# An encoder block on one core: a new order of the vector work beside the attention heads, a maximum that begins with the sink, and feed-forward values without the token's scale

## The chip, the core and the metric

The kernel runs on one core of a Trainium2 chip. A core has five engines that run their own instruction streams and wait for each other through semaphores: TensorE (PE in the profile; its weight loads are listed apart as PEld), VectorE (DVE), ScalarE (ACT), GpSimd (POOL) and SyncE (SP), which here only issues DMA transfers. The metric is the device time of one execution in microseconds (us); lower is better. Before the change it is 941.33 us, the median of three runs (941.06 to 941.93).

## The reference

One layer of a bidirectional encoder in float32: 256 tokens of width 2048, 12 query heads and 4 key/value heads of width 128, four Fourier groups, a feed-forward width of 5504. Cut to what matters:

```python
h = rmsnorm(x, norm1_g)
q, k, v, u = split(h @ w_in)
s = q @ k.T * HEAD_DIM**-0.5 - slope[head] * abs(t - s_pos)   # |t - s_pos| <= 128, else -1e30
m = maximum(max(s), sink[head])
p = exp(s - m);  p = p / (sum(p) + exp(sink[head] - m))
a = rmsnorm(p @ v, attn_out_g)
f = rmsnorm(per group: real(fft2(u)) @ w_fourier[g], fourier_out_g)
x = x + concatenate([a, f]) @ w_out

h = rmsnorm(x, norm2_g)
gate, val = split(h @ w_up)
gate = conv3(gate, dw_w) + dw_b           # over three neighbouring tokens, per channel
x = x + (gelu(gate) * val) @ w_down
y = rmsnorm(x, normf_g)
```

An rmsnorm divides each token by the root of its mean square, with 1e-6 added under the root, so a factor of a token's own that reaches the last rmsnorm drops out again, if the 1e-6 is multiplied by the square of that factor.

## The kernel before

**Precision.** Every large product is made of three: each float32 operand is cut into a high and a low part in the type fp32r, and high by high, low by high and high by low are added in PSUM. For the weights this is done while they stream in. `split` (lines 174 to 184) takes one unit of weights, 128 x 2048 numbers: ScalarE writes the high part (L181), VectorE subtracts it from the raw weights for the low part (L182), and the next unit's DMA is issued (L165, L183). There are three buffers each for raw, high and low parts.

**Order of the work.** The order is written out by hand: each engine runs its instructions in the order of the program. `unit` (line 382) is the beat: it runs what was put down as "before" unit i, then the unit's matmuls, then the "beside" list, then the split of unit i+2, then the "behind" list. "Before" holds matmuls only, so on TensorE it comes ahead of the unit's 32 large matmuls. The "beside" list holds VectorE, ScalarE and GpSimd work which in time runs next to the unit's matmuls. On these engines the split of unit i+2 stands behind the whole "beside" list of unit i.

**The stages.** First u and x are loaded and the u projection is made (to about 38 us). Then come the units for v and, from about 53 us, 16 units for keys and queries in the order k, q, q, q for each of the four key heads. In each of these, weights are held still and the tokens' parts move: 16 matmuls of 512 columns and 16 of 256 (L350). Then 16 units of the output projection (to about 251 us), then the feed-forward part.

**A head's way through the units.** If a query head is projected in unit s, then in s+1 its two halves of the PSUM bank are summed (`qk_out`, lines 629 to 636: a ScalarE copy L631 and a VectorE sum L633; for a key head also a product with the token's scale, L635) and cut into parts (`qk_parts`, L642 to 646, through `split_scaled`, L269 on ScalarE and L270 on VectorE). In s+2 TensorE makes the scores (`scores`, L654, ahead of the unit's matmuls), and `scores_out` adds the distances, takes the maximum (L670, VectorE) and makes the exponent's bias `neg` with two GpSimd instructions (L674 product with the token's scale, L675 minimum with the negated sink); `exps` (L684 to 689) follows on ScalarE in the "behind" list, with one small GpSimd sum (L689). In s+3 `weigh` divides (L694, L697), and for the first ten heads `flip_out` transposes blocks of 32 on VectorE (L314) and writes them to HBM in four DMAs (L317). In s+4 `flip_in` reads them back turned (L325). In s+6 `flip_parts` cuts them into parts (L739 ScalarE, L740 VectorE). In s+7 TensorE multiplies with v (`values`, L749), and `values_out` squares the result (L486 ScalarE), cuts it into parts (L269, L270) and adds the squares on GpSimd (L490). The last two heads are turned by TensorE instead (`turn`, `turn_out`).

**The loop that orders it** is in lines 762 to 792. In the "beside" list of one unit it puts, before the change: `flip_parts`, `weigh`, `flip_out`, `flip_in`, `qk_out`, `values_out`, `turn_out`, `scores_out`, `qk_parts`.

**Feed-forward.** Each of the 43 channel tiles has a gate and a value unit. `scaled_sum` (L922 to 926) sums the two halves of the bank and multiplies by `r2b`, the token's scale spread over a row. `gate_conv`, `gate_gelu` and `val_mult` follow. The down-projection's first 36 tiles run as five groups of seven products per column block (a Strassen-like scheme, `PRODUCTS`), whose results are added to x in `xs` by `product_out` (L1118, L1122) and `shared_out` (L1129 to 1141). The last rmsnorm's sums of squares start in `last_post` (L1159 to 1178).

Of the kernel before, what the change touches and what calls it, by code (L numbers as in the profile page):

```python
# [8 lines left out]
F32 = mybir.dt.float32  # L9
F32R = mybir.dt.float32r  # L10
AF = mybir.ActivationFunctionType
ALU = mybir.AluOpType

P = 128
D = 2048
# [3 lines left out]
NH = 12  # L19
# [7 lines left out]
EPS = 1e-6  # L27
# [11 lines left out]
V_G2, V_GA, V_GF, V_DW, V_DB, V_SINK = 0, 16, 28, 32, 161, 204  # L39
V_N = 216  # L40
# [15 lines left out]
FLIPS = range(NH - 2)  # L56
# [48 lines left out]
def block_kernel(  # L105
# [19 lines left out]
    nc = tc.nc  # L125
    SL = slopes()
# [73 lines left out]
    rel = cat_pool.tile([P, 512], F32, tag="cat", name="rel")  # L200
# [59 lines left out]
    ps = bank(dn, "ps_warm")  # L260
# [3 lines left out]
    def vcol(o, n=1):  # L264
        return vec[:, o : o + n]
# [8 lines left out]
    def rstd_of(ssq, width, name, n=2, r=None):  # L274

        var = base.tile([P, n], F32, tag="var" + name, name="var" + name)
        nc.vector.tensor_scalar(var, ssq, 1.0 / width, EPS, ALU.mult, ALU.add)
        if r is None:
            r = base.tile([P, n], F32, tag="rstd" + name, name="rstd" + name)
        nc.gpsimd.tensor_tensor(r, var, half_pow[:, 0:n], ALU.pow)  # L280
        return r
# [7 lines left out]
    def spread(r, dst, name):  # L289

        t = wp.tile([P, 512], F32, tag="junk", name=f"diag{name}")
        dgs = [t[:, b * P : (b + 1) * P] for b in range(2)]
        for b, dg in enumerate(dgs):
            nc.vector.tensor_scalar(dg, ident, r[:, b : b + 1], None, ALU.mult)
        ps = bank(dn, "ps_spread" + name)
        for b in range(2):
            nc.tensor.matmul(
                ps[:, b * P : (b + 1) * P], ones, dgs[b], start=True, stop=True
            )
        nc.vector.tensor_copy(dst, ps[:, :S])  # L300
# [72 lines left out]
    before, beside, behind = {}, {}, {}  # L373

    def at(when, i, f, *a):
        when.setdefault(i, []).append((f, a))
# [13 lines left out]
    for c in range(4):  # L390
        t = base.tile([P, 4, 512], F32R, tag=f"hT{c}", name=f"hT{c}")
        hT.append(t)
    ps_u = [bank(mm, f"ps_u{b}") for b in range(2)]
    for k in range(NK):
# [3 lines left out]
        n = 1 if c < 2 else 2  # L398
# [3 lines left out]
        if q % n == 0:  # L402
            w, h = u_part(k, 0, FW, n), hi[:, q : q + n, :]
# [20 lines left out]
    ph = pa.enter_context(tc.tile_pool(name="pa", bufs=1))  # L424
# [5 lines left out]
    rq_neg = ph.tile([P, 2], F32, tag="rq_neg", name="rq_neg")  # L430
    rq_pos = ph.tile([P, 2], F32, tag="rq_pos", name="rq_pos")
    rq_inv = ph.tile([P, 2], F32, tag="rq_inv", name="rq_inv")
    sink_neg = ph.tile([P, NH], F32, tag="sink_neg", name="sink_neg")

    def token_sums(c):
        for b in range(2):
# [150 lines left out]
    def distances():  # L587

        for b in range(2):
            s = slice(b * S, (b + 1) * S)  # L590
            nc.vector.tensor_scalar(rel[:, s], rel[:, s], rq_inv[:, b : b + 1], None, ALU.mult)
        nc.vector.tensor_scalar(sink_neg, vcol(V_SINK, NH), -1.0, None, ALU.mult)

    at(beside, 5, fourier_positions)
    at(before, 6, fourier_weights)
# [30 lines left out]
    qk_sb, st = {}, {}  # L626
    sq_a = ph.tile([P, S], F32, tag="sq", name="sq_a")

    def qk_out(kind, h, ps):
        tmp = ph.tile([P, S], F32, tag="tmp", name=f"tmp_{kind}{h}", bufs=2)  # L630
        nc.scalar.activation(tmp, ps[:, S : 2 * S], AF.Copy)  # L631
        add = ph.tile([P, S], F32, tag="add", name=f"add_{kind}{h}", bufs=2)
        nc.vector.tensor_tensor(add, ps[:, 0:S], tmp, ALU.add)  # L633
        if kind == "k":
            nc.vector.tensor_tensor(add, add, r1b, ALU.mult)  # L635
        st["add", kind, h] = add
# [25 lines left out]
    def scores_out(h):  # L662

        ps = st.pop(("s", h))
        sc = ph.tile([P, 512], F32, tag="sc", name=f"sc{h}", bufs=4)
        mx = ph.tile([P, 2], F32, tag="mx", name=f"mx{h}", bufs=2)
        neg = ph.tile([P, 2], F32, tag="neg", name=f"neg{h}", bufs=2)
        for b in range(2):
            s = slice(b * S, (b + 1) * S)
            nc.vector.tensor_tensor_reduce(  # L670
                sc[:, s], ps[:, s], rel[:, s], -float(SL[h]), -3e38, ALU.add,
                ALU.max, mx[:, b : b + 1],
            )
        nc.gpsimd.tensor_tensor(neg, mx, rq_neg, ALU.mult)  # L674
        nc.gpsimd.tensor_scalar(neg, neg, sink_neg[:, h : h + 1], None, ALU.min)  # L675
        st["sc", h] = sc, neg

    def exps(h):
# [83 lines left out]
    for i in range(N_QK, N_OUT + 8):  # L762
        heads = {i - s: h for (kind, h), s in slot_of.items() if kind == "q"}
        new = [kh for kh, s in slot_of.items() if i - s == 1]
        for n, h in sorted(heads.items()):
            if n == 5 + 2 * (h in FLIPS):
                at(before, i, values, h)
        if 4 in heads and heads[4] not in FLIPS:
            at(before, i, turn, heads[4])
        if 2 in heads:  # L770
            at(before, i, scores, heads[2])
        if 6 in heads and heads[6] in FLIPS:
            at(beside, i, flip_parts, heads[6])
        if 3 in heads:
            at(beside, i, weigh, heads[3])
            if heads[3] in FLIPS:
                at(beside, i, flip_out, heads[3])
        if 4 in heads and heads[4] in FLIPS:
            at(beside, i, flip_in, heads[4])
        for kind, h in new:  # L780
            at(beside, i, lambda k=kind, h=h: qk_out(k, h, st.pop(("ps", k, h))))
        for n, h in sorted(heads.items()):
            if n == 5 + 2 * (h in FLIPS):
                at(beside, i, values_out, h)
        if 4 in heads and heads[4] not in FLIPS:
            at(beside, i, turn_out, heads[4])
        if 2 in heads:
            at(beside, i, scores_out, heads[2])
        for kind, h in new:
            at(beside, i, qk_parts, kind, h)  # L790
        if 2 in heads:
            at(behind, i, exps, heads[2])

# [85 lines left out]
    for n, (c, kq) in enumerate(OUT_ORDER):  # L879
        i = N_OUT + n  # L880
# [39 lines left out]
    def scaled_sum(ps, name):  # L920
        tmp = fp.tile([P, S], F32, tag="ftmp", name=f"ft_{name}")
        nc.scalar.activation(tmp, ps[:, S : 2 * S], AF.Copy)  # L922
        add = fp.tile([P, S], F32, tag="fadd", name=f"fa_{name}", bufs=3)
        nc.vector.tensor_tensor(add, ps[:, 0:S], tmp, ALU.add)
        nc.vector.tensor_tensor(add, add, r2b, ALU.mult)
        sums_of[name] = add

    def gate_conv(j):
# [182 lines left out]
    def product_out(g, c, p, ps):  # L1111
        tt = nc.vector.tensor_tensor
        if p in ("P6", "P7"):
            z = Z[c, p]
            if g == 0:
                nc.scalar.activation(z, ps, AF.Copy)
            else:
                tt(z, ps, z, ALU.add)  # L1118
        else:
            n, t = {"P2": (0, 0), "N3": (1, 0), "N4": (0, 1)}[p]  # L1120
            xb = xs[2 * n + c][:, t, :]
            tt(xb, ps, xb, ALU.add)  # L1122

    def shared_out(c, step):

        p1, n5, u, p7 = held[c, "P1"], held[c, "N5"], Z[c, "P6"], Z[c, "P7"]
        x00, x10, x01, x11 = (xs[2 * n + c][:, t, :] for n in range(2) for t in range(2))
        tt = nc.vector.tensor_tensor
        if step == 0:  # L1129
            tt(u, p1, u, ALU.add)  # L1130
            tt(x00, p1, x00, ALU.add)
            w = st["w", c] = wp.tile([P, 512], F32, tag="junk", name=f"sum01_{c}")
            tt(w, n5, u, ALU.subtract)
        elif step == 1:
            tt(u, u, p7, ALU.add)
            tt(x01, x01, st["w", c], ALU.add)
            tt(x10, x10, u, ALU.add)
        else:
            w = st.pop(("w", c))
            tt(w, w, p7, ALU.subtract)  # L1140
            tt(x11, x11, w, ALU.add)

    def by_parts(ps, o, hi, lo, n, first, last):

# [14 lines left out]
    def last_post(c, b, ps, o=0, n=512):  # L1159

        xb = xs[c][:, b, o : o + n]
        nc.vector.tensor_tensor(xb, ps, xb, ALU.add)
        if c == 3:
            return
        junk = wp.tile([P, 512], F32, tag="junk", name=f"junkc{c}{b}")
        nc.scalar.activation(
            junk, xb, AF.Square, scale=D**-0.5, accum_out=ssq3[:, b, c : c + 1]
        )
        if c == 0:
            nc.vector.tensor_scalar(  # L1170
                ssq3[:, b, 3:4], ssq3[:, b, 0:1], EPS, None, ALU.add
            )
        if (c, b) == (1, 1):
            nc.gpsimd.tensor_tensor(
                ssq3[:, b, 3:4], ssq3[:, b, 3:4], ssq3[:, b, 1:2], ALU.add
            )
        if (c, b) not in ((1, 1), (2, 1)):
            nc.gpsimd.tensor_tensor(xb, xb, gfb[:, c * 512 : (c + 1) * 512], ALU.mult)
# [34 lines left out]
    for q in range(2):  # L1213
        kind, j = items[q]
# [8 lines left out]
        still_weights(hi, lo, ps, range(12, NK))  # L1223
    tot2 = base.tile([P, 2], F32, tag="tot2", name="tot2")
    nc.vector.tensor_reduce(tot2, ssq2, mybir.AxisListType.X, ALU.add)
    spread(rstd_of(tot2, D, "2"), r2b, "2")
    ff_step(1)
    up_posts(1, *items[0], pair[0][0])
    up_posts(2, *items[1], pair[1][0])
# [208 lines left out]
```

## Time and profile before

| what | value |
|---|---|
| median of three runs | 941.33 us |
| the profiled execution | 941.03 us |
| its span, first to last instruction | 938.9 us |
| busy: TensorE, VectorE, ScalarE, GpSimd | 928.0, 765.5, 539.6, 72.9 us |
| granted TensorE clock, mean over the span | 0.997 of full speed |
| memory | 223.25 MB moved, mean 238 GB/s |

The profiled execution's own time is 2.13 us more than its span; that is what lies around the instructions. In the rows of a timeline the columns are: start in us from the span's beginning, duration in us, engine, line of the kernel, operation, result and operands by the program's names, shape, how many instructions the row merges, and, in brackets, how long the engine sat idle ahead of it and for whom it waited. In a row of a group the numbers after the bar are busy time in us, the mean of one in ns, and idle time ahead of them. A row of busy time by stage gives for PE, PEld, DVE, ACT and POOL the busy us and the number of instructions, then the granted clock, the share of busy DMA engines and GB/s. Matmuls are pipelined and their ends are modelled: their starts are what was recorded, and one's end lies behind the next one's start.

### The profile page before, as it was taken

How to read it: one execution, taken by the hardware profiler on the slowest of the kernel's cores; microseconds unless marked ns; L12 is line 12 of the kernel's file. 1: busy time of each engine (PE TensorE's matmuls, PEld its weight loads, DVE VectorE, ACT ScalarE, POOL GpSimd, SP SyncE). 2: the span in 40 equal slices, each digit the busy share in tenths (PEclk: the TensorE clock that was granted, in tenths of full speed). 3: DMA queues.
4: the chain of work that ended last, by engine and by line, in shares of the span. 5: the costliest groups of instructions: out<-in, count | busy, mean ns of one | idle time of the engine just before them, and what ended most of it. 6: DMA issues, size and time to landing. Idle time of an engine off the chain costs nothing.

```text
span 938.9 us, 12849 instructions
## 1 busy us (share of the span) xinstructions
PE 928.0 (99%) x5005; PEld 803.5 (86%) x5005; DVE 765.5 (82%) x945; ACT 539.6 (57%) x672; POOL 72.9 (8%) x104
## 2 busy tenths in 40 slices
PE   9999999999999999999999999999999999999996
PEld 7888888888888888888888888888888888888885
DVE  7657888778677777798888997878979789989986
ACT  7755666645554555566555665556655556655553
POOL 0102222300000000000000000000000000000002
PEclk9999999999999999999999999999999999999998
DMA  9965767557757668887797778777787978779652
GB/s 367 309 224 169 231 196 236 193 174 281 243 221 232 177 227 238 278 269 239 220 296 252 246 216 286 237 262 232 260 248 240 309 224 269 241 233 273 194 179 90
DMA packets 55148, 223.25 MB, mean 238 GB/s; under 512 B 21136, under 2 KB 25744, under 8 KB 31536
## 3 DMA queue, kind: packets, MB, share of 16 engines
q1 hardware_dynamic: 50544, 192.94, 56.8%
q0 software_dynamic: 4544, 29.49, 16.9%
q8 instruction: 39, 0.64, 0.3%
q14 instruction: 21, 0.17, 0.1%
HBM read 216.13 MB, written 6.29 MB: 237 GB/s over the span
## 4 chain that ended last, share of the span: by engine, by line
PE 95%; DVE 2%; ACT 1%; issue 1%; DMA 0%; POOL 0%; DVEq 0%; POOLq 0%; ACTq 0%
PE ps_val L350 25%; PE ps_gate L350 25%; PE ps_q L350 5%; PE ps_P L1148 3%; PE ps_P L1149 3%; PE ps_P L1147 3%; PE ps_N L1148 3%; PE ps_N L1149 3%; PE ps_N L1147 3%; PE ps_k L350 2%; PE ps_a L333 2%; PE ps_a L335 2%; PE ps_a L334 2%; PE ps_s L654 1%; PE ps_ff L333 1%; PE ps_ff L335 1%
## 5 line engine op out<-in xcount | busy, mean ns | idle before, releaser
L182 DVE TENSOR_TENSOR lo<-raw,hi 128x2048 fp32r<-128x2048 f32 (+1 forms) x129 | 293.5, 2275 | 53.9 <-ACT hi L181 53.6
L181 ACT ACTIVATE hi<-raw 128x2048 fp32r<-128x2048 f32 (+1 forms) x129 | 245.3, 1902 | 36.7 <-PE ps_a L334 14.6
L350 PE MATMUL ps_val<-hU,hi 128*128 128x512 f32 x688 | 236.2, 389 | 0.0
L350 PE MATMUL ps_gate<-hU,hi 128*128 128x512 f32 x688 | 236.2, 389 | 0.0
L350 PE MATMUL ps_val<-hU,lo 128*128 128x256 f32 x688 | 189.9, 276 | 0.0
L350 PE MATMUL ps_gate<-hU,lo 128*128 128x256 f32 x688 | 189.9, 276 | 0.0
L350 PEld LDWEIGHTS ps_gate<-hU,hi 128*128 128x128 f32 x688 | 129.1, 188 | 26.8
L350 PEld LDWEIGHTS ps_val<-hU,hi 128*128 128x128 f32 x688 | 129.1, 188 | 26.8
L350 PEld LDWEIGHTS ps_gate<-hU,lo 128*128 128x128 f32 x688 | 129.1, 188 | 1.3
L350 PEld LDWEIGHTS ps_val<-hU,lo 128*128 128x128 f32 x688 | 129.1, 188 | 1.3
L922 ACT ACTIVATE ft_g<-ps_gate 128x256 f32<-128x256 f32 x43 | 16.5, 384 | 123.0 <-PE ps_gate L350 123.0
L922 ACT ACTIVATE ft_v<-ps_val 128x256 f32<-128x256 f32 x43 | 16.5, 384 | 91.5 <-PE ps_val L350 91.5
L350 PE MATMUL ps_q<-hT,hi 128*128 128x512 f32 x192 | 65.1, 391 | 0.0
L1147 PE MATMUL ps_P<-hi_P,op_P 128*128 128x512 f32 x144 | 56.0, 389 | 0.0
L1148 PE MATMUL ps_P<-hi_P,op_P 128*128 128x512 f32 x144 | 56.0, 389 | 0.0
L1149 PE MATMUL ps_P<-lo_P,op_P 128*128 128x512 f32 x144 | 56.0, 389 | 0.0
L350 PE MATMUL ps_q<-hT,lo 128*128 128x256 f32 x192 | 51.2, 277 | 0.0
L1039 DVE TENSOR_TENSOR lo_N<-sumw,hi_N 128x2048 fp32r<-128x2048 f32 (+1 forms) x20 | 41.5, 2077 | 9.4 <-ACT hi_N L1038 9.2
L1147 PE MATMUL ps_N<-hi_N,op_N 128*128 128x512 f32 x108 | 42.0, 389 | 0.0
L1148 PE MATMUL ps_N<-hi_N,op_N 128*128 128x512 f32 x108 | 42.0, 389 | 0.0
L1149 PE MATMUL ps_N<-lo_N,op_N 128*128 128x512 f32 x108 | 42.0, 389 | 0.0
L350 PEld LDWEIGHTS ps_q<-hT,hi 128*128 128x128 f32 x192 | 35.2, 188 | 6.6
(389 smaller groups left out, 1598.9 us busy)
## 6 DMA issues: line engine op xcount, KB each, us to landing
raw<-in_w_up SPq DMA_DIRECT2D x86, 1024.0 KB, 5.6
raw<-in_w_in SPq DMA_DIRECT2D x20, 1024.0 KB, 5.3
raw<-in_w_out SPq DMA_DIRECT2D x16, 1024.0 KB, 4.9
sumw<-in_w_down POOLq DMA_DIRECT2D x16, 1024.0 KB, 8.7
raw<-in_w_down_late SPq DMA_DIRECT2D x4, 1024.0 KB, 7.0
raw<-in_w_down_last SPq DMA_DIRECT2D x4, 768.0 KB, 4.2
turnp<-flip SPq DMA_DIRECT2D x40, 64.0 KB, 2.9
flop<-turnp SPq DMA_DIRECT2D x10, 256.0 KB, 4.7
```

Of the source, the lines that this page charges most:

```text
L181: nc.scalar.activation(hi[:, 0:n], raw[:, 0:n], AF.Copy)
L182: nc.vector.tensor_tensor(lo[:, 0:n], raw[:, 0:n], f32(hi[:, 0:n]), ALU.subtract)
L333: nc.tensor.matmul(ps, ah, wh, start=first and q == q0, stop=False)
L334: nc.tensor.matmul(ps, al, wh, start=False, stop=False)
L335: nc.tensor.matmul(ps, ah, wl, start=False, stop=last and q == q0 + len(kk) - 1)
L350: nc.tensor.matmul(ps[:, x], (hi, lo)[i][:, k * P : (k + 1) * P], hk(k)[:, x], start=n == 0 and k == 0, stop=n == len(order) - 1 and k == ...
L654: nc.tensor.matmul(ps[:, b * S : (b + 1) * S], qT[:, qo + b * P : qo + (b + 1) * P], kT[:, ko : ko + S], start=n == 0, stop=n == 2,)
L922: nc.scalar.activation(tmp, ps[:, S : 2 * S], AF.Copy)
L1039: nc.vector.tensor_tensor(lo, src, f32(hi), ALU.subtract)
L1147: nc.tensor.matmul(ps, o[:, 0, p, :], hi[:, s], start=first and p == 0, stop=False)
L1148: nc.tensor.matmul(ps, o[:, 1, p, :], hi[:, s], start=False, stop=False)
L1149: nc.tensor.matmul(ps, o[:, 0, p, :], lo[:, s], start=False, stop=last and p == n - 1)
```

## The change

Four things are done.

- **The "beside" list of a head's unit is put in a new order:** `qk_out`, `flip_parts`, `qk_parts`, `values_out`, `weigh`, `flip_out`, `flip_in` or `turn_out`, `scores_out`.
- **The maximum begins with the sink.** The running maximum of L670 started from -3e38; now it starts from the sink divided by the query scale, which is computed once per block of 128 tokens in `distances` (two small products in place of one). The minimum on GpSimd falls away, and the product with the negated scale moves from GpSimd to VectorE.
- **Feed-forward values keep the token's scale out.** The product with `r2b` is made for gates only. What is then added to x is larger by the token's root mean square, `rms2`, so x is multiplied by it once, in the first group's `product_out` (six instructions) and in the last step of `shared_out` (two), with an instruction that multiplies and adds in one. The 1e-6 of the last rmsnorm is multiplied by the square of `rms2` (`eps3`).
- **The new small results lie in columns 216 to 231 of the tile `vec`,** which were not in use, and in a tile that has the size and place of the one that falls away.

```diff
-    sink_neg = ph.tile([P, NH], F32, tag="sink_neg", name="sink_neg")
+    sink_least = [ph.tile([P, NH], F32, tag="sink0", name="sink0"), vcol(V_N, NH)]
...
-        nc.vector.tensor_scalar(sink_neg, vcol(V_SINK, NH), -1.0, None, ALU.mult)
+        for b in range(2):
+            nc.vector.tensor_scalar(
+                sink_least[b], vcol(V_SINK, NH), rq_inv[:, b : b + 1], None, ALU.mult
+            )
...
             nc.vector.tensor_tensor_reduce(
-                sc[:, s], ps[:, s], rel[:, s], -float(SL[h]), -3e38, ALU.add,
-                ALU.max, mx[:, b : b + 1],
+                sc[:, s], ps[:, s], rel[:, s], -float(SL[h]), sink_least[b][:, h : h + 1],
+                ALU.add, ALU.max, mx[:, b : b + 1],
             )
-        nc.gpsimd.tensor_tensor(neg, mx, rq_neg, ALU.mult)
-        nc.gpsimd.tensor_scalar(neg, neg, sink_neg[:, h : h + 1], None, ALU.min)
+        nc.vector.tensor_tensor(neg, mx, rq_neg, ALU.mult)
...
+        for kind, h in new:
+            at(beside, i, lambda k=kind, h=h: qk_out(k, h, st.pop(("ps", k, h))))
         if 6 in heads and heads[6] in FLIPS:
             at(beside, i, flip_parts, heads[6])
+        for kind, h in new:
+            at(beside, i, qk_parts, kind, h)
+        for n, h in sorted(heads.items()):
+            if n == 5 + 2 * (h in FLIPS):
+                at(beside, i, values_out, h)
         if 3 in heads:
             at(beside, i, weigh, heads[3])
             if heads[3] in FLIPS:
                 at(beside, i, flip_out, heads[3])
-        if 4 in heads and heads[4] in FLIPS:
-            at(beside, i, flip_in, heads[4])
-        for kind, h in new:
-            at(beside, i, lambda k=kind, h=h: qk_out(k, h, st.pop(("ps", k, h))))
-        for n, h in sorted(heads.items()):
-            if n == 5 + 2 * (h in FLIPS):
-                at(beside, i, values_out, h)
-        if 4 in heads and heads[4] not in FLIPS:
-            at(beside, i, turn_out, heads[4])
+        if 4 in heads:
+            at(beside, i, flip_in if heads[4] in FLIPS else turn_out, heads[4])
         if 2 in heads:
             at(beside, i, scores_out, heads[2])
-        for kind, h in new:
-            at(beside, i, qk_parts, kind, h)
...
-        nc.vector.tensor_tensor(add, add, r2b, ALU.mult)
+        if name[0] == "g":
+            nc.vector.tensor_tensor(add, add, r2b, ALU.mult)
...
-            tt(xb, ps, xb, ALU.add)
+            if g == 0:
+                nc.vector.scalar_tensor_tensor(xb, xb, rms2[:, t : t + 1], ps, ALU.mult, ALU.add)
+            else:
+                tt(xb, ps, xb, ALU.add)
...
-            tt(x11, x11, w, ALU.add)
+            nc.vector.scalar_tensor_tensor(x11, x11, rms2[:, 1:2], w, ALU.mult, ALU.add)
...
-                ssq3[:, b, 3:4], ssq3[:, b, 0:1], EPS, None, ALU.add
+                ssq3[:, b, 3:4], ssq3[:, b, 0:1], eps3[:, b : b + 1], None, ALU.add
...
-    spread(rstd_of(tot2, D, "2"), r2b, "2")
+    r2 = rstd_of(tot2, D, "2")
+    spread(r2, r2b, "2")
+    rms2, eps3 = vcol(V_N + NH, 2), vcol(V_N + NH + 2, 2)
+    nc.vector.reciprocal(rms2, r2)
+    nc.vector.tensor_tensor(eps3, rms2, rms2, ALU.mult)
+    nc.vector.tensor_scalar(eps3, eps3, EPS, None, ALU.mult)
```

## The prediction, made before the changed kernel ran

> **What bounds the kernel now.** I read the page's busy times first, then the list of waits for TensorE, then busy time by stage, then TensorE's own timeline around the attention heads.
>
> ```profile
> PE 928.0 (99%) x5005; PEld 803.5 (86%) x5005; DVE 765.5 (82%) x945; ACT 539.6 (57%) x672; POOL 72.9 (8%) x104
> ...
> PE ps_s L654 <- ACT qT L269: 1.4, 2, 0.9
> ...
> sum 650.00, PE 650.00 PEld 564.55 DVE 555.42 ACT 372.39 POOL 26.42; mean PE 162.50 PEld 141.14 DVE 138.85 ACT 93.10 POOL 6.61
> ```
>
> The first line says that TensorE works all the time: work taken from another engine is worth only what TensorE waits for that engine. The second is the one wait that TensorE has in the heads' units: twice, 1.4 us together, for the high part of a query (`qT`, L269). The third sums the feed-forward stages from 263 to 913 us: TensorE is busy 650.00 us of 650.00. So no edit in that part can bring anything by way of VectorE, and the whole question is what TensorE loses in the heads' units. The idle column is too coarse for that, since matmul ends are modelled; the starts tell it.
>
> ```profile
> 90.12 0.71 PE L350 MATMUL ps_q<-hT,hi 128*128 128x512 f32 x2
> 95.73 1.21 PE L654 MATMUL ps_s<-kT,qT 128*128 128x256 f32 x6
> 96.78 0.63 PE L350 MATMUL ps_q<-hT,hi 128*128 128x512 f32 x2
> ...
> 109.87 0.88 PE L654 MATMUL ps_s<-kT,qT 128*128 128x256 f32 x6
> 110.59 0.62 PE L350 MATMUL ps_q<-hT,hi 128*128 128x512 f32 x2
> 116.04 0.40 PE L749 MATMUL ps_o<-pt,v_hi 128*128 128x256 f32 x2
> 116.75 0.63 PE L350 MATMUL ps_q<-hT,hi 128*128 128x512 f32 x2
> 122.94 1.19 PE L654 MATMUL ps_s<-kT,qT 128*128 128x256 f32 x6 [0.54 <-ACT qT L269]
> 123.97 0.63 PE L350 MATMUL ps_q<-hT,hi 128*128 128x512 f32 x2
> ...
> 143.93 0.63 PE L350 MATMUL ps_q<-hT,hi 128*128 128x512 f32 x2
> 150.43 1.20 PE L654 MATMUL ps_s<-kT,qT 128*128 128x256 f32 x6 [0.85 <-ACT qT L269]
> 151.47 0.61 PE L350 MATMUL ps_q<-hT,hi 128*128 128x512 f32 x2
> ```
>
> Undisturbed, a unit's 32 matmuls take 116.04 - 110.59 = 5.45 us, a head's scores 110.59 - 109.87 = 0.72 us and its values 116.75 - 116.04 = 0.71 us. Against this:
>
> - from 116.75 the unit takes 6.19 us to the scores' start (0.74 too much), and the scores take 1.03 us (0.31 too much): 1.05 us;
> - from 143.93 it takes 6.50 us (1.05 too much), and the scores 1.04 us (0.32 too much): 1.37 us;
> - the scores at 95.73 take 1.05 us: 0.33 us. Their unit is 0.16 us long too, but it stands behind narrow matmuls, so I leave that out.
>
> Together **2.75 us**. Why it happens is in VectorE's beat, the low part of the weights that ends each unit's list:
>
> ```profile
> 110.15 2.30 DVE L182 TENSOR_TENSOR lo<-raw,hi 128x2048 fp32r<-128x2048 f32 x1 [0.88 <-ACT hi L181]
> ...
> 117.93 2.29 DVE L182 TENSOR_TENSOR lo<-raw,hi 128x2048 fp32r<-128x2048 f32 x1 [0.87 <-ACT hi L181]
> ...
> 124.72 2.29 DVE L182 TENSOR_TENSOR lo<-raw,hi 128x2048 fp32r<-128x2048 f32 x1 [1.38 <-ACT hi L181]
> ...
> 130.31 2.29 DVE L182 TENSOR_TENSOR lo<-raw,hi 128x2048 fp32r<-128x2048 f32 x1 [1.27 <-ACT hi L181]
> ...
> 137.63 2.29 DVE L182 TENSOR_TENSOR lo<-raw,hi 128x2048 fp32r<-128x2048 f32 x1 [0.88 <-ACT hi L181]
> ```
>
> Four units (one key head and its three queries) take VectorE 137.63 - 110.15 = 27.48 us, of which it sits idle 0.87 + 1.38 + 1.27 + 0.88 = 4.40 us for ScalarE's high part. TensorE needs only 4 x 5.45 + 3 x 0.72 + 3 x 0.71 = 26.09 us. VectorE thus falls behind by 1.39 us in four units, and once in four units TensorE waits about that long (1.05 and 1.37 us).
>
> **The change, part by part.**
>
> *New order.* One unit of the timelines of ScalarE and VectorE shows the knot:
>
> ```profile
> 119.16 0.36 ACT L631 ACTIVATE tmp_q<-ps_q 128x256 f32<-128x256 f32 x1
> 119.42 0.37 ACT L486 ACTIVATE sq<-ps_o 128x256 f32<-128x256 f32 x1
> 119.69 0.46 ACT L269 ACTIVATE cat<-ps_o,vec 128x256 fp32r<-128x256 f32 x1
> ...
> 122.05 0.39 DVE L633 TENSOR_TENSOR add_q<-ps_q,tmp_q 128x256 f32<-128x256 f32 x1
> 122.36 0.47 DVE L270 SCALAR_TENSOR_TENSOR cat<-ps_o,vec,cat 128x256 fp32r<-128x256 f32 x1
> 122.47 0.42 ACT L269 ACTIVATE qT<-add_q 128x256 fp32r<-128x256 f32 x1 [2.32 <-DVE add_q L633]
> 122.79 1.90 ACT L181 ACTIVATE hi<-raw 128x2048 fp32r<-128x2048 f32 x1
> 122.92 0.42 DVE L270 SCALAR_TENSOR_TENSOR qT<-add_q,qT 128x256 fp32r<-128x256 f32 x1
> ```
>
> The copy that the sum needs is done at 119.16 + 0.36 = 119.52, and VectorE's low part at 117.93 + 2.29 = 120.22. But the sum starts at 122.05, since weighing and transposing another head stand ahead of it. ScalarE idles 2.32 us for it, its high part of the weights (122.79) comes as much later, and VectorE idles for that in turn. With the sum first it starts at 120.22. The high part of the query follows 0.42 us behind a sum (122.47 - 122.05) and takes 0.42 us: done at 121.06. The low part follows 0.87 us behind the sum and takes 0.42: done at 121.51. TensorE comes for them at 116.75 + 5.45 = 122.20. So this wait is gone with 1.1 us to spare, even with the lag as it stands, and the first matmul that reads the low part is later still.
>
> The lag goes too. ScalarE then does the two instructions for the values (119.42 and 119.69, 0.37 + 0.46 us at most) and starts the weights at about 121.9 instead of 122.79; VectorE, with its own work pulled together, is free at about 123.3 and waits about 0.4 us in place of 1.38. In units with scores it has more work of its own and should not wait. I take 0.4 us of the 4.40 as left.
>
> *The maximum.* `neg` is one more VectorE instruction per head, of which before has no row; two GpSimd instructions go. The nearest row is the reciprocal of the same 128 x 2 shape:
>
> ```profile
> L694 DVE RECIPROCAL ex<-sm 128x2 f32<-128x2 f32 x12 | 1.9, 160 | 2.6 <-POOL sm L689 2.2
> ...
> L490 POOL TENSOR_TENSOR sq_a<-sq_a,sq 128x256 f32<-128x256 f32 x11 | 10.2, 930 | 9.6 <-ACT sq L486 9.5
> ...
> 131.71 0.94 POOL L689 TENSOR_TENSOR sm<-sm,ex 128x2 f32<-128x2 f32 x1 [2.24 <-ACT ex L688]
> ...
> 174.64 0.20 POOL L689 TENSOR_TENSOR sm<-sm,ex 128x2 f32<-128x2 f32 x1 [1.58 <-ACT ex L688]
> ```
>
> I take 0.2 us each, 0.6 us in four units; its bounds are 0.16 (the row) and 0.42 (a 256-column instruction above). That L670 starts from a column and not from a constant also has no row: between nothing and 0.16 us more for each of six instructions in four units, up to 1.0 us; I take nothing, as it is one more operand and not one more instruction. VectorE's four units become 27.48 - 4.0 + 0.6 = 24.1 us (at worst 25.7), still under TensorE's 26.09. So VectorE keeps step, and **2.75 us** go; the next to set the pace is TensorE itself. Behind `neg` on VectorE is queued the weights' low part, 0.2 us later; TensorE wants it two units on. The exponentials wait for `neg` as before, for one instruction in place of two.
>
> *What moves with the order.* Transposing, the four writes to HBM and the read back come later by the sum, the parts and the values' instruction ahead of them now, 0.39 + 0.42 + 0.47 = 1.28 us. On SP's queue their order, and that of the weights' load behind them, stays.
>
> ```profile
> flop<-turnp SPq DMA_DIRECT2D x10, 256.0 KB, 4.7
> ...
> 124.11 0.41 SPq L325 DMA_DIRECT2D flop<-turnp  x1
> ...
> 138.86 0.71 ACT L739 ACTIVATE pt<-flop 128x256 fp32r<-128x256 f32 x2
> ```
>
> A read back issued at 124.11 lands at 128.8 and is used at 138.86: 10.1 us of cover, of which 1.28 are spent. Cost nothing. The load of the next weights waits for VectorE's low part anyway.
>
> *Feed-forward.*
>
> ```profile
> L925 DVE TENSOR_TENSOR fa_v<-fa_v,r2b 128x256 f32<-128x256 f32 x43 | 18.3, 425 | 1.5
> ...
> 264.09 2.28 DVE L182 TENSOR_TENSOR lo<-raw,hi 128x2048 fp32r<-128x2048 f32 x1
> ...
> 269.00 0.39 PE L350 MATMUL ps_val<-hU,hi 128*128 128x512 f32 x1
> ```
>
> 43 products leave VectorE, 18.3 us, and TensorE's 650.00 of 650.00 us hide all of it: **nothing**. Three small instructions come in behind the spread scale, 0.6 us at 0.2, ahead of a low part that ends at 266.37 and is used at 269.00: covered four times over. Eight additions become multiply-and-add, one for one, in place of far more that goes. Behind the last matmul only one operand of one small sum changes. Nothing.
>
> **Sum.** 2.75 us, round 2.8, off the profiled execution's 941.03 us (span 938.9, so 936.1 after). The median of the runs shown lies 0.30 us above that execution, so I forecast 941.33 - 2.8 = **938.5 us**, 0.3% less.
>
> **Rivals.**
>
> *Only the idle column is real.* It has 0.54 + 0.85 = 1.39 us at the two scores, half of my sum. Then 941.33 - 1.39 = 939.9 us. For it: it is what the list of waits says. Against it: starts are recorded and ends modelled, and the scores' own 0.3 us excess is inside "busy". The Trainium skill, "Trainium Kernel Development and Optimization", section Performance Expectations, calls matmul busy time a bad metric because matmuls are pipelined. By that the starts are to be read; the trace agrees, with 2.75 us against 1.39.
>
> *GpSimd holds up VectorE.* A GpSimd sum of 128 x 2 takes 0.20 us alone (174.64) and 0.94 us when it starts within VectorE's low part of 130.31: it ends at 132.65, with it, at 132.60. So the two do shut each other out. The sums of squares (L490, 0.93 us) now run while VectorE has the query's low part or the weighing to do; if each held it up fully, that is 3 x 0.93 = 2.8 us in four units: 24.1 + 2.8 = 26.9, 0.8 us more than TensorE's 26.09. Over the three stretches that lose time now, some 2.4 us stay: 941 us. Against it: these sums also ran beside the same engine before. The Trainium skill, "SBUF — State Buffer", section Who interferes with whom, says that a VectorE instruction with two SBUF inputs and a GpSimd instruction that reads SBUF exclude each other, the later one waiting for the other's end. The sum of 131.71 agrees with it.
>
> *The change doesn't do what it says:* the wait moves, for instance to the copy that ScalarE can make only behind the exponentials, and TensorE stays as late: 941.3 us. Against it: that copy is done 0.7 us before VectorE is free for the sum (119.52 against 120.22).
>
> *Slower: the read back from HBM comes late.* `flip_parts` now stands between the sum and the query's low part, on ScalarE and VectorE alike, so a late `flop` would hold up the next scores. It decides from the point where the 8.8 us of cover left are used up; each half microsecond beyond costs 0.5 us for ten heads, 5 us, less the 2.8: 943.5 us. Against it: the cover is almost twice the transfer's 4.7 us.
>
> **How the numbers follow.** Forecast 0.78; idle column 0.07; GpSimd 0.05; wait moves 0.06; read back late 0.04. The forecast's own width is what I left out or rounded (0.16 us at 90.12, the median's 0.3 us against the profile): 937.9 to 939.2. The range goes on to the first rival's 939.9. About 0.2%, 1.9 us, is what a measurement of this kernel can tell from no change; the line is at 939.45 us. Faster by more: the forecast, 0.78. Within: the first three rivals, 0.18. Slower: 0.04.
>
> **What would show it.** In the new profile every head's scores take 0.72 us from start to start and every unit 5.45 to 5.55; the wait for `qT` on TensorE is gone; ScalarE's idle time for the sum (L633) falls from over 2 us to a few tenths; VectorE's idle time for the weights' high part in four units falls from 4.40 to below 1 us. The feed-forward stages take as long as before, to 0.1 us, with VectorE some 18 us less busy. It is wrong if TensorE waits anywhere for the query's parts, if the feed-forward part moves, or if the time behind the last matmul changes.

## The result, and the profile after

| what | before | after |
|---|---|---|
| median, runs side by side on one chip | 941.13 us (8 runs, 940.36 to 941.93) | 938.19 us (8 runs, 938.08 to 939.15) |
| ratio | | 0.9972, 95% interval 0.9961 to 0.9982 |
| profiled execution, and its span | 941.03, 938.9 us | 938.08, 936.3 us |
| first scores (`ps_s`) to first tile of the output's second half (`ps_ff`) | 70.75 to 185.47: 114.72 us | 70.99 to 182.99: 112.00 us |
| start of the last matmul | 930.29 us | 927.66 us |

The changed kernel is 0.28% faster (0.18 to 0.39%). The fourth row is the one to work with: the stretch holds all the heads' work from the first scores on, its ends are starts of matmuls, and it became 2.72 us shorter. Up to the first scores the changed kernel was 0.24 us later, and behind the stretch it was 0.15 us shorter (744.67 against 744.82 us to the last matmul), so the last matmul starts 2.63 us sooner.

First the page's busy times and TensorE's list of waits, of the changed kernel:

```profile
PE 926.8 (99%) x5005; PEld 803.6 (86%) x5005; DVE 750.0 (80%) x918; ACT 540.9 (58%) x672; POOL 62.2 (7%) x80
```

```profile
PE ps_warm L262 <- POOL ones L254: 1.0, 1, 1.0
PE ps_u L412 <- ACT hT L269: 0.2, 1, 0.2
```

VectorE is 15.5 us less busy and the time falls by 3: still only what TensorE waits for counts. The two waits left are at the kernel's start. The one for a query's high part (`qT`, 1.4 us before) is gone. The feed-forward stages, busy time by stage, columns as before:

```profile
sum 650.00, PE 650.00 PEld 564.87 DVE 538.91 ACT 371.48 POOL 26.38; mean PE 162.50 PEld 141.22 DVE 134.73 ACT 92.87 POOL 6.59
```

VectorE has 16.5 us less to do there (538.91 against 555.42; some 18 were forecast) and TensorE is as full as before. Next TensorE's timeline in the heads' units (lines moved by the change: scores are L657, values L751):

```profile
109.71 0.88 PE L657 MATMUL ps_s<-kT,qT 128*128 128x256 f32 x6
110.43 0.62 PE L350 MATMUL ps_q<-hT,hi 128*128 128x512 f32 x2
...
115.88 0.40 PE L751 MATMUL ps_o<-pt,v_hi 128*128 128x256 f32 x2
...
116.60 0.63 PE L350 MATMUL ps_q<-hT,hi 128*128 128x512 f32 x2
...
122.08 0.88 PE L657 MATMUL ps_s<-kT,qT 128*128 128x256 f32 x6
122.79 0.63 PE L350 MATMUL ps_q<-hT,hi 128*128 128x512 f32 x2
...
128.27 0.40 PE L751 MATMUL ps_o<-pt,v_hi 128*128 128x256 f32 x2
```

From 116.60 the unit takes 122.08 - 116.60 = 5.48 us (6.19 before) and its scores 0.71 us (1.03 before). No head's unit between 83 and 156 us now shows more than 5.55 us, and none of the scores more than 0.72. VectorE's beat, and the knot on VectorE:

```profile
107.10 0.16 DVE L677 TENSOR_TENSOR neg<-mx,rq_neg 128x2 f32<-128x2 f32 x1
107.18 2.29 DVE L182 TENSOR_TENSOR lo<-raw,hi 128x2048 fp32r<-128x2048 f32 x1
109.61 0.42 DVE L636 TENSOR_TENSOR add_k<-ps_k,tmp_k 128x256 f32<-128x256 f32 x1
...
114.47 2.29 DVE L182 TENSOR_TENSOR lo<-raw,hi 128x2048 fp32r<-128x2048 f32 x1
116.68 0.42 DVE L636 TENSOR_TENSOR add_q<-ps_q,tmp_q 128x256 f32<-128x256 f32 x1
...
125.42 2.29 DVE L182 TENSOR_TENSOR lo<-raw,hi 128x2048 fp32r<-128x2048 f32 x1 [0.29 <-ACT hi L181]
...
133.36 2.30 DVE L182 TENSOR_TENSOR lo<-raw,hi 128x2048 fp32r<-128x2048 f32 x1
```

Four units take 133.36 - 107.18 = 26.18 us, TensorE's own pace (26.09 by the prediction's sum), in place of 27.48. Of the 4.40 us of idling for the weights' high part, 0.29 are left. The list of VectorE's waits in that stretch gives what idle time it now has, and for whom:

```profile
DVE add_q L636 <- ACT tmp_q L634: 1.6, 2, 1.2
DVE qT L270 <- ACT qT L269: 0.5, 1, 0.5
DVE lo L182 <- ACT hi L181: 0.3, 1, 0.3
DVE cat L270 <- ACT cat L269: 0.2, 1, 0.2
```

That is 2.6 us in four units: VectorE has become the engine that waits.

So far all is as forecast. But the forecast gave the whole of it to the new order alone, and that could be tried.

### The profile page after: what moved, and what is told of

The parts are those of the page before. It is cut to its first block, busy times and chain, and to the rows that moved or that the text cites. A ratio compares the mean times of both kernels' runs of the same rounds, so it can differ in the third digit from the quotient of the medians.

```text
span 936.3 us, 12803 instructions
## 1 busy us (share of the span) xinstructions
PE 926.8 (99%) x5005; PEld 803.6 (86%) x5005; DVE 750.0 (80%) x918; ACT 540.9 (58%) x672; POOL 62.2 (7%) x80
## 3 DMA queue, kind: packets, MB, share of 16 engines
q0 software_dynamic: 4544, 29.49, 16.5%
## 4 chain that ended last, share of the span: by engine, by line
PE 98%; DVE 1%; DMA 0%; ACT 0%; issue 0%; DVEq 0%; POOLq 0%; POOL 0%; ACTq 0%
PE ps_val L350 25%; PE ps_gate L350 25%; PE ps_q L350 7%; PE ps_P L1151 3%; PE ps_P L1152 3%; PE ps_P L1153 3%; PE ps_N L1151 3%; PE ps_N L1153 3%; PE ps_N L1152 3%; PE ps_a L335 2%; PE ps_k L350 2%; PE ps_a L333 2%; PE ps_a L334 2%; PE ps_s L657 1%; PE ps_o L751 1%; PE ps_ff L333 1%
## 5 line engine op out<-in xcount | busy, mean ns | idle before, releaser
L922 ACT ACTIVATE ft_g<-ps_gate 128x256 f32<-128x256 f32 x43 | 16.5, 384 | 124.6 <-PE ps_gate L350 124.6
L922 ACT ACTIVATE ft_v<-ps_val 128x256 f32<-128x256 f32 x43 | 16.5, 383 | 92.5 <-PE ps_val L350 92.5
```

## The experiments

Each time stands beside its own runs of the kernel before on the same chip. "Stretch" is the time from the first `ps_s` to the first `ps_ff`, read from the starts as above (before 114.72, after 112.00 us). Where the diff keeps the old maximum, lines up to the loop are those of before; else those of the changed kernel.

### One part at a time

**The order alone:** the loop as in the change, all else as before.

> The kernel before with the new order of the beside list alone; the maximum and the feed-forward part as before. My theory (VectorE's beat in the heads' units is longer than TensorE's, since the sum stands late and holds up ScalarE's high part of the weights): the whole gain, 2.75 us against before, so a ratio of 0.997, no wait of TensorE for the query's parts, and VectorE's idle time for the high part of the weights in four units down from 4.4 us to about 0.5. Rival (the shorter way from the maximum to the exponentials does it): the time of before. Rival (the 18 us of vector work that leave the feed-forward part do it): the time of before.

Measured: 943.1 us against 941.19, ratio 1.0024 (1.0015 to 1.0033). Stretch 117.18 us, 2.46 **longer**. The expectation fell. The trace shows why. One unit of it, VectorE, GpSimd and ScalarE together:

```profile
108.85 0.42 DVE L670 CUSTOM_DVE_ANT_0 sc<-ps_s,rel 128x256 f32<-128x256 f32 x1
109.19 0.08 DVE L670 DVE_READ_ACCUMULATOR2_ANT mx<- 128x1 f32 x1
109.19 2.29 DVE L182 TENSOR_TENSOR lo<-raw,hi 128x2048 fp32r<-128x2048 f32 x1
109.36 2.18 POOL L674 TENSOR_TENSOR neg<-mx,rq_neg 128x2 f32<-128x2 f32 x1 [4.11 <-DVE mx L670]
111.64 0.28 POOL L675 TENSOR_SCALAR neg<-neg,sink_neg 128x2 f32<-128x2 f32 x1
111.95 0.60 ACT L684 ACTIVATE sc<-sc,neg,rq_pos 128x256 f32<-128x256 f32 x1 [3.53 <-POOL neg L675]
...
113.32 0.36 ACT L631 ACTIVATE tmp_k<-ps_k 128x256 f32<-128x256 f32 x1
...
113.72 0.42 DVE L633 TENSOR_TENSOR add_k<-ps_k,tmp_k 128x256 f32<-128x256 f32 x1 [2.24 <-ACT tmp_k L631]
```

With the sum early, VectorE is never idle at the end of its list: it goes from the maximum straight into the weights' low part (109.19). GpSimd's product of 128 x 2 numbers begins 0.17 us behind it and ends at 111.54, with the low part (111.48). The exponentials follow at 111.95, the copy for the next sum stands behind them, and VectorE idles 2.24 us for that copy. The idling for the weights' high part did fall as expected, to 0.60 us in four units, but VectorE now idles 4.4 us in them for the copies, and the four units take it 28.19 us (109.19 to 137.38). In the kernel before, the same two steps were quick, because something else stood between the maximum and the weights' low part: first the low part of a query, which takes only 0.42 us, then VectorE's idle time (until 110.15 and 130.31, as the prediction's rows of the beat show). One row of VectorE's timeline, and GpSimd's:

```profile
108.85 0.42 DVE L270 SCALAR_TENSOR_TENSOR qT<-add_q,qT 128x256 fp32r<-128x256 f32 x1
...
109.01 0.31 POOL L674 TENSOR_TENSOR neg<-mx,rq_neg 128x2 f32<-128x2 f32 x1 [3.56 <-DVE mx L670]
109.42 0.28 POOL L675 TENSOR_SCALAR neg<-neg,sink_neg 128x2 f32<-128x2 f32 x1
...
128.78 0.31 POOL L674 TENSOR_TENSOR neg<-mx,rq_neg 128x2 f32<-128x2 f32 x1 [7.82 <-DVE mx L670]
129.19 0.28 POOL L675 TENSOR_SCALAR neg<-neg,sink_neg 128x2 f32<-128x2 f32 x1
```

The list of ScalarE's waits gives the whole (first before, then the order alone):

```profile
ACT sc L684 <- POOL neg L675: 3.6, 1, 3.6
```

```profile
ACT sc L684 <- POOL neg L675: 26.8, 8, 3.5
```

So I formed a new theory: **the order pays only if the small steps behind the maximum are not on GpSimd while VectorE does its two-operand low part**, and that is what the other edit brings.

**The maximum alone.**

> The kernel before with the new maximum alone (it begins with the sink, one VectorE product in place of two GpSimd instructions). My theory: slower than before, since VectorE, which is already the late engine here, gets 0.2 us more for each of three heads in four units, and up to 0.1 us for the two maxima: 0.6 to 0.9 us in four units, over the two to three stretches that lose time, 1.2 to 2.5 us more, 942.3 to 943.6 us. Rival (the shorter way to the exponentials does it): 938.4 us. Third: no difference, if ScalarE's earlier start at the exponentials makes up for it.

Measured: 940.57 us, ratio 0.9993 (0.9984 to 1.0002), stretch 114.71 us. My theory's time didn't come, but the third alternative did: without the order this edit neither costs nor brings anything that can be told from nothing.

**The feed-forward edits alone.**

> The kernel before with the feed-forward edit alone (values without the token's scale, x multiplied by the root mean square, the last 1e-6 scaled). My theory: the time of before within 0.3 us, and TensorE's stretch from the first feed-forward unit to the last matmul as long as before to 0.1 us, though VectorE is 18 us less busy. Rival (the freed vector work shortens it): 938.4 us or less.

Measured: 940.92 us, ratio 0.9997 (0.9988 to 1.0006), stretch 114.72 us. As expected: nothing.

**The sum moved to the front of the list, all else as before** (`qk_out` first, `qk_parts` still last).

> The kernel before with one thing moved: the sum (its ScalarE copy, its VectorE sum, the product for keys) to the front of the beside list; the cut into parts stays last. My theory, that the beat counts: ScalarE no longer waits for the sum, so the weights' high part comes early, VectorE's beat falls to about 24 us in four units as with the whole order, and all of 2.75 us go: 938.4 us. Rival, that only the early parts of the query count, since the scores wait for them: the low part still stands last on VectorE and the scores go on waiting for it, so half of the gain at most, 939.7 to 941.1 us.

Measured: 940.87 us, ratio 0.9999 (0.9990 to 1.0008), stretch 114.17 us. The expectation fell, and the time lies in the range of its rival: only 0.55 us of the 2.72 go, and scores still take 1.61 us at 121.96 and 2.04 us at 148.99. In the heads' units TensorE now waits for the low part of a query alone:

```profile
PE ps_s L654 <- DVE qT L270: 1.7, 2, 1.1
```

Two things make it late, and this run doesn't separate them. One is the rival's: the low part still stands last in VectorE's list, behind weighing and transposing; ahead of the scores at 121.96 the sum starts at 120.02 and the low part only at 122.53. The other is GpSimd: with a query's low part between the maximum and the weights the product is just quick enough and the second step is shut out, so that the exponentials, the copy and the sum at 120.02 are late too (VectorE idles 1.95 us for that copy). Its GpSimd timeline:

```profile
106.48 0.31 POOL L674 TENSOR_TENSOR neg<-mx,rq_neg 128x2 f32<-128x2 f32 x1 [3.56 <-DVE mx L670]
106.89 2.20 POOL L675 TENSOR_SCALAR neg<-neg,sink_neg 128x2 f32<-128x2 f32 x1
```

### Is it GpSimd's place?

**Order and new maximum together, feed-forward as before.**

> New order and new maximum together, feed-forward as before the change. Theory (VectorE's low part shuts GpSimd's small steps out for 2.2 us, and the new maximum takes them away): the whole gain is in these two together, 938.2 to 938.5 us; `neg` stands on VectorE and the exponentials wait for it 1.1 us a head or less; no wait of TensorE for `qT`. Rival (the parts only add, order +1.9 us, maximum -0.6, feed-forward -0.3 by their single runs): 942.2 to 942.6 us, the new order's loss staying.

Measured: 938.2 us against 941.13, ratio 0.9969 (0.9957 to 0.9981), stretch 112.00 us. That is the whole gain. By stretches the order alone costs 2.46 us and the maximum alone brings 0.01; together they bring 2.72. The two edits do not add.

**The same, but the one small step that is left goes back to GpSimd.** The feed-forward part is that of before here, unlike what the expectation says. Against the run with order and maximum:

```diff
-        nc.vector.tensor_tensor(neg, mx, rq_neg, ALU.mult)
+        nc.gpsimd.tensor_tensor(neg, mx, rq_neg, ALU.mult)
```

> As the run with order and maximum, and with the changed feed-forward part, but the one product `neg` that is left stays on GpSimd. Theory (GpSimd is shut out by the low part that VectorE begins right behind the maximum): the product takes some 2.2 us in most of the units as the two steps did, the exponentials and the copy behind them come that late, and the time is 941 to 943 us. Rival (what counts is that there is one step and not two, or that the maximum begins with the sink): the product takes 0.2 to 0.3 us and the time is 938.2 to 938.5 us.

Measured: 939.85 us, ratio 0.9986 (0.9978 to 0.9995), stretch 113.50 us. The mechanism is there, in its GpSimd timeline:

```profile
108.26 2.12 POOL L677 TENSOR_TENSOR neg<-mx,rq_neg 128x2 f32<-128x2 f32 x1 [4.29 <-DVE mx L673]
...
117.07 2.11 POOL L677 TENSOR_TENSOR neg<-mx,rq_neg 128x2 f32<-128x2 f32 x1 [2.40 <-DVE mx L673]
...
128.87 0.19 POOL L677 TENSOR_TENSOR neg<-mx,rq_neg 128x2 f32<-128x2 f32 x1 [5.86 <-DVE mx L673]
```

Where VectorE's low part begins at once (108.04, 116.84) the same product takes 2.1 us; where VectorE idles 0.48 us ahead of it (for the high part, until 129.28) it takes 0.19. This single edit gives back 1.50 of the 2.72 us (113.50 against 112.00). My size was too high (941 to 943): TensorE's list of waits has `qT` only once, 0.8 us, at 149.55, while the beat of 135.69 - 108.04 = 27.65 us first uses up the lead that the early sum gives. That the lead is the reason was not tried by itself.

**The order, with the old maximum, and both small steps on VectorE.** Here too the feed-forward part is that of before, unlike what the expectation says. Against the order alone:

```diff
-        nc.gpsimd.tensor_tensor(neg, mx, rq_neg, ALU.mult)
-        nc.gpsimd.tensor_scalar(neg, neg, sink_neg[:, h : h + 1], None, ALU.min)
+        nc.vector.tensor_tensor(neg, mx, rq_neg, ALU.mult)
+        nc.vector.tensor_scalar(neg, neg, sink_neg[:, h : h + 1], None, ALU.min)
```

> New order, changed feed-forward part, the maximum as before from -3e38, and both small steps behind it (the product and the minimum with the sink) on VectorE. Theory (only GpSimd's place is at fault): one more small VectorE instruction a head, 0.16 to 0.42 us, is covered by the 2.55 us that VectorE idles in four units: 938.1 to 938.8 us. Rival (the start with the sink, or one step less in the chain, is what pays): 940.5 to 943 us.

Measured: 938.09 us, ratio 0.9969 (0.9958 to 0.9981), stretch 112.00 us. Moving two small steps to another engine takes the order alone from 943.1 us to 938.1. The start with the sink isn't needed; that the steps leave GpSimd is enough.

**The order alone, with the maximum earlier in the list.** This one takes the collision away and leaves both steps on GpSimd, the old maximum and the old feed-forward part. Against the order alone:

```diff
+        if 2 in heads:
+            at(beside, i, scores_out, heads[2])
         if 3 in heads:
             at(beside, i, weigh, heads[3])
...
-        if 2 in heads:
-            at(beside, i, scores_out, heads[2])
```

> New order, with the old maximum, both small steps on GpSimd and feed-forward as before the change; only the scores' maximum stands elsewhere: ahead of the weighing and the transposing, and no longer at the end of the list. Theory (the small steps are slow only where VectorE's two-operand low part starts right behind the maximum): behind the maximum VectorE now has one-operand work, so the two steps take 0.2 to 0.3 us each in units with a head to weigh and transpose, the exponentials come early, and the time is 938.1 to 939 us with GpSimd's work left where it was. Rival (GpSimd's steps cost by their number and by the passing from engine to engine, wherever they stand): 941 to 943 us, as with the order alone.

Measured: 937.73 us against 940.99, ratio 0.9965 (0.9951 to 0.9978), stretch 112.00 us. The group rows of the two GpSimd steps, in this kernel:

```profile
L675 POOL TENSOR_SCALAR neg<-neg,sink_neg 128x2 f32<-128x2 f32 x12 | 4.5, 378 | 1.2
...
L674 POOL TENSOR_TENSOR neg<-mx,rq_neg 128x2 f32<-128x2 f32 x12 | 2.5, 211 | 33.6 <-DVE mx L670 20.9 <-DVE ex L694 12.7
```

With the order alone the means were 1381 and 444 ns; here 211 and 378, with the same instructions on the same engine. Behind the maximum VectorE now divides and transposes, in short instructions (a row of VectorE's timeline, two of GpSimd's):

```profile
105.44 0.62 DVE L697 TENSOR_SCALAR sc<-sc,ex 128x256 f32<-128x256 f32 x2
...
105.40 0.20 POOL L674 TENSOR_TENSOR neg<-mx,rq_neg 128x2 f32<-128x2 f32 x1 [3.92 <-DVE ex L694]
105.70 0.43 POOL L675 TENSOR_SCALAR neg<-neg,sink_neg 128x2 f32<-128x2 f32 x1
```

The product takes what it takes beside an idle VectorE. The minimum takes 0.43 us in place of 0.28 and ends with the two divisions (106.13 and 106.06), so the division holds GpSimd up as well, but not for long. From the order alone, 943.1 us, one moved call takes it to 937.7. Against the changed kernel no difference can be told (the intervals overlap and the stretches are equal).

### How much room VectorE has

**The change, with two or four more VectorE instructions a unit** behind the list of units 10 to 25:

```diff
+    def more_vector():
+        for n in range(2):
+            r = rel[:, n % 2 * S : (n % 2 + 1) * S]
+            nc.vector.tensor_tensor(r, r, r, ALU.max)
...
+        if N_QK + 2 <= i < N_OUT + 2:
+            at(beside, i, more_vector)
```

(the second kernel has `range(4)`).

> The changed kernel with two more VectorE instructions of 128 x 256 (a maximum of a tile with itself, which changes nothing) behind the list of each unit from 10 to 25: some 0.7 us a unit, 2.7 us in four units of a key head. VectorE idles 2.55 us in four units, so by the theory of the beat (its work must stay under TensorE's 26.1 us) next to nothing shows: 938.2 to 939.2 us. Rival (whatever delays the high and low parts delays TensorE, with no slack): up to 0.7 us for each of 11 units with a head's work, 944 to 946 us.

Measured: 938.8 us against 941.13, ratio 0.9974 (0.9963 to 0.9984), stretch 112.01 us: nothing. VectorE's four units take 26.46 us (109.36 to 135.82), and it no longer waits for the high part in any of them.

> The changed kernel with four more VectorE instructions of 128 x 256 behind the list of each unit from 10 to 25. Theory of the beat: VectorE's work in four units is 26.18 - 2.55 = 23.6 us and grows by 5.5 us to 29.1, 2.9 us over TensorE's 26.2; over 16 units some 11.6 us, less the lead that VectorE has at the start (2 to 4 us) and what it makes up in units without a head: 944 to 948 us. Rival (VectorE still has room, as two instructions a unit showed nothing): 938 to 940 us.

Measured: 945.61 us against 940.99, ratio 1.0047 (1.0035 to 1.0060), stretch 119.59 us. The changed kernel's four units and this one's, as busy time by stage (PE, PEld, DVE, ACT, POOL):

```profile
107.18:133.36 26.18, 26.18 (x166) 23.64 (x165) 22.89 (x51) 18.26 (x39) 4.44 (x6) 1.00 0.73 224
```

```profile
112.81:141.96 29.15, 27.37 (x167) 24.12 (x166) 27.87 (x66) 18.05 (x41) 8.08 (x6) 1.00 0.67 201
```

The beat came out at 29.15 us where the sum gave 29.1, and TensorE waits for it (`qT`, 1.74 us at 124.33 alone). So the sum by beats holds: a beat of 26.46 us still costs nothing and one of 29.15 does. Where between the two doses the loss begins was not tried; the 2.6 us of idle time agree with it.

## Why the prediction was right, and which step was wrong

**Right: the sum.** TensorE lost 2.75 us in the heads' units by the starts; the stretch became 2.72 us shorter, and every unit and score has the length that was named undisturbed. Starts and not idle times had to be counted: the list of waits had 1.4 us, so the rival of the idle column falls.

**Right: the beat.** 26.09 us were named for TensorE, and VectorE's beat is 26.18; 0.4 us of idling for the high part were left in the estimate, and 0.29 are. The run with four more instructions confirms that VectorE's work against TensorE's 26.1 us in four units decides.

**Partly right: ScalarE's wait for the sum.** It was to fall from over 2 us a time to a few tenths. ScalarE's list of waits has the totals of before and of after:

```profile
ACT qT L269 <- DVE add_q L633: 27.4, 12, 3.0
```

```profile
ACT qT L269 <- DVE add_q L636: 7.3, 7, 1.8
```

It is a quarter in sum, but 1.0 us each time that it still occurs; the parts were in time all the same.

**Right within the noise: nothing in the feed-forward part**, by its own run and by 650.00 of 650.00 us. From its first matmul (`ps_gate`, 251.30 before, 248.82 after) to the last it is 0.15 us shorter, 678.84 against 678.99, a little more than the 0.1 that was named; the kernel with the order alone, which lacks these edits, has 678.77, so this is no effect of theirs that could be told. The read back from HBM isn't late either: TensorE's list has no wait for `pt`, so the rival that would have ended slower doesn't occur in the changed kernel. And nothing moved behind the last matmul: from 930.29 to the span's end at 938.9 it is 8.6 us, and from 927.66 to 936.3 it is 8.6 us.

**Wrong: "The exponentials wait for `neg` as before, for one instruction in place of two."** That step, and the part on the new order, which let the order alone take the 2.75 us. "As before" is what fails: the two GpSimd steps were short only because the low part of a query and VectorE's idle time stood between the maximum and the weights' low part, and the order takes just these away. With the order alone ScalarE waits 26.8 us for `neg` in place of 3.6, and the kernel is 1.9 us slower than before. This is the rival "the wait moves, for instance to the copy that ScalarE can make only behind the exponentials". I gave it 0.06 and argued against it with the copy's time in the old trace, where the exponentials weren't late. But once they were, and I overlooked it: the 3.6 us in the list of ScalarE's waits are the last head's, with no query behind it, where the weights' low part follows the maximum at once. These are rows of the kernel before:

```profile
170.34 2.29 DVE L182 TENSOR_TENSOR lo<-raw,hi 128x2048 fp32r<-128x2048 f32 x1
...
170.50 2.18 POOL L674 TENSOR_TENSOR neg<-mx,rq_neg 128x2 f32<-128x2 f32 x1 [2.17 <-DVE mx L670]
```

The new order makes this one case the rule: with the order alone one of the two steps takes about 2.2 us in 8 of the 12 heads. The edit that I priced as a cost of 0.6 us in four units is thus the one that lets the order pay. In the changed kernel the wait is there too, but short: 8.7 us over 8 heads, for `neg` on VectorE.

**Sizes of the maximum's edit.** `neg` takes 161 ns by its group row (0.2 taken, 0.16 the lower bound); the maximum takes 458 and 480 ns (417 before), so the column as a start costs 0.04 to 0.06 us each where I took nothing. From the first maximum to the low part it is 114.47 - 113.50 = 0.97 us against 109.19 - 108.53 = 0.66 with the order alone: 0.31 us a head, 0.9 in four units against the 0.6 taken. VectorE's 2.6 us of room cover it.

**The rival on GpSimd had the engines the wrong way round for the new order.** I cited the Trainium skill, "SBUF — State Buffer", section Who interferes with whom: a VectorE instruction with two SBUF inputs and a GpSimd instruction that reads SBUF exclude each other, and the later one waits for the other's end. I weighed it only for GpSimd holding VectorE up. With the new order it is the other direction that costs: the low part begins 0.17 us ahead, and a product of 0.19 to 0.31 us lasts 2.18. By that rule the second case could have been seen ahead; the trace agrees with it, as a step that begins behind the weights' low part takes 2.1 to 2.2 us and ends 0.05 to 0.15 us after it. What the runs themselves show is the dependence on what VectorE does at that moment; that a shared port is the means is the Trainium skill's word.

The direction that I weighed is there too, but in the kernel before, and it cost time there. I argued only that these sums "also ran beside the same engine before". Rows of that kernel, from VectorE's timeline and GpSimd's:

```profile
106.19 0.62 DVE L697 TENSOR_SCALAR sc<-sc,ex 128x256 f32<-128x256 f32 x2
...
112.70 1.01 POOL L490 TENSOR_TENSOR sq_a<-sq_a,sq 128x256 f32<-128x256 f32 x1 [0.20 <-ACT sq L486]
...
113.23 0.90 DVE L697 TENSOR_SCALAR sc<-sc,ex 128x256 f32<-128x256 f32 x2
```

A head's two divisions take 0.61 to 0.62 us where no such sum is running, and 0.86 to 0.99 where one is: in 7 of the 12 heads before, in 1 of 12 in the changed kernel. With the order alone it is none. So the new order takes some 0.8 us off VectorE in the four units that the prediction summed, and that sum leaves it out.

So the number was right for a sum that holds, with half of its mechanism missing. Had the change been the order alone, the same argument would have forecast 938.5 us for a kernel of 943.1.

## What to carry to other kernels

When an edit takes idle time away from an engine, ask who was using that idle time: a short step on GpSimd, quick in the old trace, may be so only because VectorE stands still, or does something short, beside it. A small step on the way to the next stage belongs on the engine that made its input, or that engine should go on with short instructions and not with a long one that has two SBUF operands; here either was enough. Look through the old trace for a single case that already has the new neighbours: here it was the last head. And count what the bounding engine loses by starts, per unit and against an undisturbed unit; then a beat of VectorE under that of TensorE tells how much more can be put in.

## What the runs showed of the hardware

- Beside an idle VectorE, GpSimd's product of 128 x 2 numbers took 0.19 to 0.20 us and its minimum 0.28 to 0.30. The product took 0.31 us beside a query's low part of 0.42 us, and either took 2.1 to 2.2 us when it began just behind a VectorE `TENSOR_TENSOR` of 2.29 us on 128 x 2048 numbers from SBUF; the wait shows as GpSimd's own duration, not as idle time.
- VectorE's one-operand division of 128 x 256 (24 of them) took 433 ns in the mean before, 352 with the order alone and 366 in the changed kernel, without any edit to it. The slow ones are those that stand beside a running GpSimd sum of 128 x 256: a pair took 0.86 to 0.99 us there and 0.61 to 0.62 elsewhere. GpSimd's minimum took 0.42 to 0.43 us in turn when it began within a division.
- A maximum that begins with a column of SBUF took 458 to 480 ns where one that begins with a constant took 417.
